# Four late tiles of layer 0's feed-forward as block products, with their sums on VectorE

## The chip, the cores and the metric

The kernel runs on one core of a Trainium2 chip. The time is the device time of one execution, in microseconds; of several executions the median counts. The profile is of one execution of its own. The engines are called by their names or by the profile's letters: TensorE (PE; its weight loads are PEld), VectorE (DVE), ScalarE (ACT), GpSimd (POOL) and SyncE (SP), whose queue issues most loads from memory.

## The reference, cut to what matters

The program computes one step of a network of two layers over 640 tokens (128 of context, 512 of the sample) with 1024 features. Each layer is a mixer (gated DeltaNet in layer 0, neighbourhood attention in layer 1) and then a gated feed-forward network. The change touches the feed-forward network of layer 0 alone:

```python
def conv_ffn(h, w_up, conv_w, conv_b, w_down):
    u = dwconv_centred(h @ w_up, conv_w) + conv_b
    val, gate = jnp.split(u, 2, axis=-1)
    return (jax.nn.silu(gate) * val) @ w_down
```

`w_up` is 1024 x 5632 (2816 value and 2816 gate columns), the convolution has three taps along the tokens, `w_down` is 2816 x 1024. The input `h` is normalised and modulated; modulation vectors of both layers come from a conditioning vector times a matrix.

## The kernel before, in words

Features lie on the 128 partitions and tokens along them, so a tile is 128 features by 640 tokens. Every matrix product is done in three passes (`pass3`, L394 to L396): each operand is split into a rounded high part and the rest (low), and high x high, high x low and low x high are added up. So every weight tile is cast to its high half on ScalarE (L382, `wh...`) and its low half is the difference, made on VectorE (L384, `wl...`). The two halves go to buffers with the tags `wh` and `wl`, two of each; loads land in a ring of two buffers, `wst`.

**The feed-forward loop (`ffn`)** goes over 22 tiles of 128 hidden features. A direct tile (`dense_pair`) computes a value tile (`duv`) and a gate tile (`dug`): 8 blocks of input features, in token pieces of 384 and 256 columns, three passes each, so 48 matmuls for each of the two. Then ScalarE and VectorE do the convolution (L454, L460), silu (L676), the product of both (L677) and the split of the result into the buffer F (L679, L680).

**Block products (`pair`).** In layer 1 the tiles 8, 10, 12, 14, 16, 18 and 20 are computed otherwise. Value and gate weights and the halves of the tokens and input features are seen as 2 x 2 blocks, and the product is made of seven block products instead of eight (Strassen's scheme in Winograd's form): seven times 4 blocks x 3 passes of 320 columns, 84 matmuls. Their order is 5, 1, 6, 3, 2, 7, 4. Sums of weight blocks (L600, L603, L604, L607, 512 columns each) and two sums of results (L610, L617, 320 columns) are on GpSimd; five sums that read a result from PSUM (L609, L612, L614, L616, L619) are on VectorE. Each of the seven weight operands is split by `quarter` (L552 on ScalarE, L553 on VectorE, 512 columns); two of them share one buffer of the tags `wh` and `wl`. Sums of the input's blocks are needed once per layer: `blocks` makes them in eight steps, which write the tiles T0 to T3; `TSTEP` says behind which tile each step is traced.

**Down products (`downs`).** After groups of tiles (`GROUPS`) the partial down projection (`rdn`) of the group is added to the residual X: eight output tiles, two token pieces each, three VectorE updates (L485) per output tile. The last group goes through `into_residual_split`, which keeps the weights of six output tiles over both token pieces (`hold`). In layer 0 the groups have 8, 7 and 7 tiles, in layer 1 they have 6, 5, 5 and 6. A group's products are traced after the tile behind it: with groups up to 8 and 15, after tiles 8 and 15.

**Modulation sums (`ada_rows`).** In layer 0's loop 64 parts are done beside the tiles: a load on GpSimd's queue (`adr`, L240, three buffers) and two multiply-and-reduce instructions on VectorE (L258) each. `SUMS[0]` says how many are traced behind each tile: none behind tile 0, then 3. The loop also issues, on GpSimd's queue, the copies that make layer 1's attention mask and bias (`rows`).

**Order.** A planner orders each engine's instructions: among those that it takes to be ready, the one traced first goes first, so a later one is pulled ahead where the engine would be idle. Each engine then works its queue in that order and waits where an operand or buffer isn't there. `high_priority` moves instructions ahead (residual updates by 300), and `chained` keeps TensorE's order as traced.

Of the kernel before, what the change touches and what calls it, by code (L numbers as in the profile page):

```python
# [13 lines left out]
F32R = mybir.dt.float32r  # L14
# [10 lines left out]
W = 640  # L25
# [29 lines left out]
ALIGN = 32, 32  # L55
SHIFT = 448
ADB = 3
GROUPS = (((0, 8), (8, 15), (15, 22)), ((0, 6), (6, 11), (11, 16), (16, 22)))
FB = 9, 7
NH = W // 2  # L60
BYBLOCK = ((), (8, 10, 12, 14, 16, 18, 20))
TSTEP = (3, 4, 4, 5, 5, 6, 6, 7)
SUMS = ((0,) + (3,) * 21, (0, 3, 3, 3, 3, 2, 2))

SEGS = ((0, PC, PC + 128, 1), (0, SC, SC + 256, 0), (1, SC + 256, SC + 512, 0))

# [26 lines left out]
class Net:  # L93
# [483 lines left out]
    def pair(self, l, i, fp, pf):  # L577

        nc, a = self.nc, self.a
        P, V = nc.gpsimd.tensor_tensor, nc.vector.tensor_tensor  # L580
        g = fp.tile([128, KT * 128], F32, tag="wsg", name=f"wsg{l}{i}", bufs=1)
        nc.sync.dma_start(g, a["w_up"][l, NFT + i])
        v = self.wp.tile([128, KT * 128], F32, tag="wst", name=f"wsv{l}{i}", bufs=WSTB)
        self.load = nc.sync.dma_start(v, a["w_up"][l, i]).ins
        v0, v1, g0, g1 = v[:, :512], v[:, 512:], g[:, :512], g[:, 512:]
        s1, s2 = (fp.tile([128, 512], F32, tag=t, name=f"{t}{l}{i}", bufs=1) for t in ("s1", "s2"))
        first, last = (lambda k: (self.hh[:, k], self.hl[:, k])), (lambda k: (self.hh[:, k + 4], self.hl[:, k + 4]))
        L, R = (0, NH), (NH, W)
# [12 lines left out]
        x = product(5, s1, self.tmov(0), L)
        nc.scalar.copy(p5, x)
        P(s2, s1, v0, ALU.subtract)  # L603
        P(g0, v0, g0, ALU.subtract)  # L604
        x = product(1, v0, first, L)
        nc.scalar.copy(p1, x)
        P(s1, v1, s2, ALU.subtract)  # L607
        x = product(6, s2, self.tmov(1), L)
        V(cg1, x, p1, ALU.add)  # L609
        P(cv1, cg1, p5, ALU.add)  # L610
        x = product(3, s1, last, R)
        V(cv1, x, cv1, ALU.add)  # L612
        x = product(2, v1, last, L)
        V(cv0, x, p1, ALU.add)  # L614
        x = product(7, g0, self.tmov(2), L)
        V(cg0, x, cg1, ALU.add)  # L616
        P(cg1, cg0, p5, ALU.add)  # L617
        x = product(4, g1, self.tmov(3), L)
        V(cg0, x, cg0, ALU.add)  # L619
        self.spare = None  # L620
        return [(0, W, cv)], [(0, W, cg)]

    def downs(self, l, grp, fs):

        g0, g1 = GROUPS[l][grp]
        n = g1 - g0
        for m in range(KT):
            w = self.weights(self.a["w_dn"][l, m][:, g0 * 128 : g1 * 128], n, f"dn{l}{grp}{m}")
            for half, c in enumerate(HALVES_R):
                ps = self.half_bank(f"rdn{l}{grp}{m}{half}", 0, half)  # L630
                self.prod(ps, -c[0], w, n, lambda k: (fs[g0 + k][:, 0], fs[g0 + k][:, 1]), c)
                with self.tc.high_priority(HP):
                    self.residual(ps, m, half, l, 5, -c[0])

    def ffn(self, l, fp, pf, norm, norms, between=None):
        nc, a = self.nc, self.a
        self.align(fp, SHIFT)
        fcw = self.smv("fcw").rearrange("p (l t w) -> p l t w", l=2, w=3)[:, l]
        fcb = self.smv("fcb").rearrange("p (l t) -> p l t", l=2)[:, l]
        last = len(GROUPS[l]) - 1  # L640

        def hold(name, n):
            if not BYBLOCK[l]:
                if name[-1] == "5":
                    return fp.tile([128, 2 * W], F32R, tag="F", name=name, bufs=FB[l])[:, 16 : 16 + n]
                return fp.tile([128, n], F32R, tag=name[:2] + name[-1], name=name, bufs=1)
            j = 2 * int(name[-1]) + (name[1] == "l")
            if j // 3 not in held:
                held[j // 3] = fp.tile([128, 2560], F32R, tag=f"T{j // 3}", name=f"Th{l}{j // 3}", bufs=1)
            o = 16 + 768 * (j % 3)  # L650
            return held[j // 3][:, o : o + n]

        g, d = (self.pa, "g", 3), (pf, "d", 5)
        direct = ((d, d), (d, d))
        self.banks = [g, d]
        if BYBLOCK[l]:
            self.T = [fp.tile([128, 2560], F32R, tag=f"T{j}", name=f"T{j}{l}", bufs=1) for j in range(4)]
            self.T = [t.rearrange("p (k a c) -> p k a c", k=4, a=2) for t in self.T]
        steps = self.blocks(fp, l)
        fs, held = {}, {}  # L660
        after = {g1: grp for grp, (_, g1) in enumerate(GROUPS[l][:-1])}
        for i in range(NFT):
            names = [f"uv{l}{i}", f"ug{l}{i}"]
            grp = after.get(i)
            if i not in BYBLOCK[l]:
                up = [a["w_up"][l, i], a["w_up"][l, NFT + i]]
                with self.behind(self.marks if i == 0 else ()):
                    pv, pg = self.dense_pair(up, names, direct, norm if i == 0 else None)
            else:
                pv, pg = self.pair(l, i, fp, pf)  # L670
            with self.tc.high_priority(FHP if i == NFT - 1 else 0):
                yv = fp.tile([128, W], F32, tag="yv", name=f"yv{l}{i}", bufs=2)
                yg = fp.tile([128, W], F32, tag="yg", name=f"yg{l}{i}", bufs=2)
                self.conv_parts(yv, pv, fcw[:, i], fcb[:, i : i + 1])
                self.conv_parts(yg, pg, fcw[:, NFT + i], fcb[:, NFT + i : NFT + i + 1])
                nc.scalar.activation(yg, yg, AF.Silu)  # L676
                nc.vector.tensor_tensor(yv, yv, yg, ALU.mult)  # L677
                f = fp.tile([128, 2 * W], F32R, tag="F", name=f"F{l}{i}", bufs=FB[l]).rearrange("p (a w) -> p a w", a=2)
                nc.scalar.copy(f[:, 0], yv)  # L679
                nc.vector.tensor_tensor(f[:, 1], yv, f[:, 0].bitcast(F32), ALU.subtract)  # L680
            fs[i] = f
            for _ in range(TSTEP.count(i) if BYBLOCK[l] else 0):
                next(steps, None)
            if between:
                between(i)
            if grp is not None:
                self.downs(l, grp, fs)
        self.spare = None
        g0, g1 = GROUPS[l][last]
        srcs = [a["w_dn"][l, m][:, g0 * 128 : g1 * 128] for m in range(KT)]  # L690
        movs = lambda k: (fs[g0 + k][:, 0, :], fs[g0 + k][:, 1, :])
        norm = self.into_residual_split(srcs, g1 - g0, movs, l, 5, f"dn{l}{last}", norms, hold, (6, 7))
        self.banks = None
        return norm
# [919 lines left out]
def build(ctx, tc, a):  # L1614
# [33 lines left out]
    with tc.tile_pool(name="fp0", bufs=2, reuse_waits="tile") as fp, ps_ffn(0) as pf:  # L1648
# [31 lines left out]
    with tc.tile_pool(name="fp1", bufs=2, reuse_waits="tile") as fp, ps_ffn(1) as pf:  # L1680
# [100 lines left out]
```

## Time and profile before

| | |
|---|---|
| median of three executions | 1844.83 us (1844.82, 1844.83, 1848.35) |
| the profiled execution | 1847.01 us, its span 1845.1 us |
| mean granted TensorE clock | 0.987 of full speed |
| layer 0's feed-forward, first direct matmul to the last group's first | 575.72 to 983.55 us |
| layer 1's feed-forward, the same | 1378.31 to 1791.95 us |
| TensorE busy, 575 to 984 us | 125.93 of 126, 55.00 of 55, 97.00 of 97, 48.00 of 48, 83.00 of 83 us |
| VectorE busy in the same stretches | 120.75, 51.93, 69.78, 21.58, 51.98 us |
| GpSimd busy in the same stretches | 21.35, 12.99, 9.41, 0.00, 0.00 us |

The stretches are tiles 0 to 8, the first group, tiles 9 to 15, the second group, and tiles 16 to 21. Rows of the profile begin with the line of the kernel or with the time from the span's start; a row of an instruction has its duration behind its start, then engine, line, operation, what it writes `<-` what it reads, the shapes, and in square brackets how long its engine was idle before it and what ended that. A busy time is the union of the instructions' durations; successive VectorE instructions overlap by about 0.1 us, so their durations add up to more.

### The profile page before, as it was taken

The page shows a single profiled execution, that of the slowest core. Times are in us where ns is not written, and L with a number is a line of the kernel's source. Part 1 is how long each engine was busy: PE and PEld are TensorE (multiplying, and loading weights), DVE is VectorE, ACT ScalarE, POOL GpSimd, SP SyncE. Part 2 cuts the span into 40 slices and gives each one's busy share as a digit, 9 for nine tenths or more (in the row PEclk, how much of TensorE's full clock was granted, in tenths as well). Part 3 has the DMA queues.
Part 4 walks back from the last instruction along what each step waited for, and adds up shares of the span by engine and source line. Part 5 has one row for each costly group of instructions (what it writes and reads, how often), then busy time and mean ns, then how long its engine had stood idle before and what let it go on. Part 6 is the DMA issues. An engine that isn't in the chain of part 4 may idle for free.

```text
span 1845.1 us, 34889 instructions
## 1 busy us (share of the span) xinstructions
PE 1774.2 (96%) x13503; PEld 1684.9 (91%) x13503; DVE 1368.7 (74%) x3445; ACT 772.0 (42%) x1606; POOL 333.4 (18%) x524
## 2 busy tenths in 40 slices
PE   6889999988999999999999999999999999999998
PEld 5878988887989999999999988888899999999998
DVE  6797868686668999965466899555679967678585
ACT  4453444254534432243233434444445424344353
POOL 0255103107003112200000212111041002032110
PEclk9999999999999999999999999999999999999999
DMA  7223233322242445542223354222233221222231
GB/s 303 74 74 110 54 126 107 100 68 79 56 160 85 154 145 174 171 157 71 80 79 93 127 153 141 76 75 68 86 128 121 86 86 63 87 71 83 79 99 60
DMA packets 103638, 194.19 MB, mean 105 GB/s; under 512 B 39624, under 2 KB 59162, under 8 KB 100712
## 3 DMA queue, kind: packets, MB, share of 16 engines
q1 hardware_dynamic: 94528, 161.57, 27.8%
q0 software_dynamic: 8400, 29.87, 5.1%
q8 instruction: 106, 1.74, 0.4%
q14 instruction: 60, 0.49, 0.1%
q10 hardware_dynamic: 544, 0.52, 0.1%
HBM read 183.09 MB, written 12.46 MB: 106 GB/s over the span
## 4 chain that ended last, share of the span: by engine, by line
PE 73%; DVE 12%; DMA 4%; issue 4%; ACT 3%; POOL 3%; SPq 1%; POOLq 0%; DVEq 0%; ACTq 0%
PE rdn L396 5%; PE rdn L394 5%; PE rdn L395 5%; PE duv L396 5%; PE duv L394 4%; PE duv L395 4%; PE dug L394 4%; PE dug L396 4%; PE dug L395 4%; PE p L982 1%; PE rgo L394 1%; PE rgo L395 1%; POOL lY L953 1%; PE rgo L396 1%; DVE nt L349 1%
## 5 line engine op out<-in xcount | busy, mean ns | idle before, releaser
L396 PE MATMUL rdn<-F,wldn 128*128 128x384 f32 (+1 forms) x632 | 193.8, 307 | 0.5 <-DVE wldn L384 0.5
L394 PE MATMUL rdn<-F,whdn 128*128 128x384 f32 (+1 forms) x632 | 193.8, 307 | 0.0
L395 PE MATMUL rdn<-F,whdn 128*128 128x384 f32 (+1 forms) x632 | 193.5, 306 | 0.0
L396 PE MATMUL duv<-hh,wluv 128*128 128x384 f32 (+1 forms) x592 | 182.0, 307 | 3.6 <-DVE wluv L384 3.6
L394 PE MATMUL duv<-hh,whuv 128*128 128x384 f32 (+1 forms) x592 | 181.5, 307 | 0.0
L395 PE MATMUL duv<-hl,whuv 128*128 128x384 f32 (+1 forms) x592 | 181.5, 307 | 0.0
L395 PE MATMUL dug<-hl,whug 128*128 128x384 f32 (+1 forms) x592 | 181.0, 306 | 0.0
L394 PE MATMUL dug<-hh,whug 128*128 128x384 f32 (+1 forms) x592 | 181.0, 306 | 0.0
L396 PE MATMUL dug<-hh,wlug 128*128 128x384 f32 (+1 forms) x592 | 181.0, 306 | 0.0
L485 DVE SCALAR_TENSOR_TENSOR X<-rdn,mods,X 128x128 f32<-128x128 f32 (+1 forms) x168 | 67.9, 435 | 79.2 <-PE rdn L396 79.0
L396 PEld LDWEIGHTS rdn<-F,wldn 128*128 128x128 f32 x632 | 118.8, 188 | 1.4 <-DVE wldn L384 1.4
L394 PEld LDWEIGHTS rdn<-F,whdn 128*128 128x128 f32 x632 | 118.6, 188 | 0.0
L395 PEld LDWEIGHTS rdn<-F,whdn 128*128 128x128 f32 x632 | 118.6, 188 | 0.0
L396 PEld LDWEIGHTS duv<-hh,wluv 128*128 128x128 f32 x592 | 111.1, 188 | 6.0 <-DVE wluv L384 5.9
L395 PEld LDWEIGHTS duv<-hl,whuv 128*128 128x128 f32 x592 | 111.2, 188 | 0.1
L396 PEld LDWEIGHTS dug<-hh,wlug 128*128 128x128 f32 x592 | 111.2, 188 | 0.0
L394 PEld LDWEIGHTS duv<-hh,whuv 128*128 128x128 f32 x592 | 111.2, 188 | 0.0
L394 PEld LDWEIGHTS dug<-hh,whug 128*128 128x128 f32 x592 | 111.1, 188 | 0.0
L395 PEld LDWEIGHTS dug<-hl,whug 128*128 128x128 f32 x592 | 111.1, 188 | 0.0
L460 DVE SCALAR_TENSOR_TENSOR yv<-duv,sm,yv 128x127 f32<-128x127 f32 (+1 forms) x222 | 86.8, 432 | 15.4 <-ACT yv L454 14.5
L382 ACT CAST whdn<-wstdn 128x896 fp32r<-128x896 f32 (+3 forms) x50 | 43.5, 869 | 126.9 <-PE rdn L395 102.4
L460 DVE SCALAR_TENSOR_TENSOR yg<-dug,sm,yg 128x127 f32<-128x127 f32 (+1 forms) x222 | 86.6, 432 | 9.1 <-ACT yg L454 8.3
(763 smaller groups left out, 5346.7 us busy)
## 6 DMA issues: line engine op xcount, KB each, us to landing
adat<-w_ada SPq DMA_DIRECT2D x20, 1024.0 KB, 5.4
adr<-w_adar POOLq DMA_DIRECT2D x80, 256.0 KB, 3.1
wstuv<-w_up SPq DMA_DIRECT2D x37, 512.0 KB, 3.5
wstug<-w_up SPq DMA_DIRECT2D x37, 512.0 KB, 3.5
adr<-w_adar SPq DMA_DIRECT2D x32, 256.0 KB, 2.8
wstdn<-w_dn SPq DMA_DIRECT2D x16, 448.0 KB, 3.3
wstdn<-w_dn SPq DMA_DIRECT2D x16, 384.0 KB, 3.1
wstdn<-w_dn SPq DMA_DIRECT2D x16, 320.0 KB, 2.9
```

The source lines that it names most:

```text
L349: nc.vector.scalar_tensor_tensor(t[:, :n], self.X[:, k, c0:c1], scg[:, k, v : v + 1], rs[:, c0 - base : c1 - base], ALU.mult, ALU.mult)
L382: nc.scalar.copy(wh[:, c], st[:, c])
L394: nc.tensor.matmul(out, a, mh, start=first, stop=False)
L395: nc.tensor.matmul(out, a, ml, start=False, stop=False)
L396: ins = nc.tensor.matmul(out, b, mh, start=False, stop=last).ins
L460: nc.vector.scalar_tensor_tensor(y[:, a:b], t[:, a + sh - lo : b + sh - lo], wv[:, tap : tap + 1], y[:, a:b], ALU.mult, ALU.add,)
L485: nc.vector.scalar_tensor_tensor(x, ps[:, base + c0 : base + c1], self.mod(l, gi, m, v), x, ALU.mult, ALU.add)
L953: eng.tensor_tensor(Y[:L, :i, lo:hi], Y[:L, :i, lo:hi], pr, ALU.add)
L982: nc.tensor.matmul(out, lhsT, rhs, start=True, stop=True, tile_position=(r, c))
```

## The change

In layer 0 the tiles 14, 16, 18 and 20 become block products too. For them all sums, those of weight blocks and of results, are on VectorE; in layer 1 GpSimd keeps its six. The eight steps of `blocks` are traced in layer 0 behind tiles 10, 10, 11, 11, 12, 12, 13 and 13. Layer 0's groups become those of layer 1 (6, 5, 5 and 6 tiles), so one group more; its F buffers go from nine to seven, and its held low and high halves of the last group go into the tiles T0 to T3, as in layer 1, instead of into tags of their own. The modulation sums of layer 0 are traced as 0, 5, 5 and then 4 behind each tile. Layer 1 computes as before.

```diff
-GROUPS = (((0, 8), (8, 15), (15, 22)), ((0, 6), (6, 11), (11, 16), (16, 22)))
-FB = 9, 7
+GROUPS = ((0, 6), (6, 11), (11, 16), (16, 22))
+FB = 7
-BYBLOCK = ((), (8, 10, 12, 14, 16, 18, 20))
-TSTEP = (3, 4, 4, 5, 5, 6, 6, 7)
-SUMS = ((0,) + (3,) * 21, (0, 3, 3, 3, 3, 2, 2))
+BYBLOCK = ((14, 16, 18, 20), (8, 10, 12, 14, 16, 18, 20))
+TSTEP = ((10, 10, 11, 11, 12, 12, 13, 13), (3, 4, 4, 5, 5, 6, 6, 7))
+SUMS = ((0, 5, 5) + (4,) * 19, (0, 3, 3, 3, 3, 2, 2))
...
     def pair(self, l, i, fp, pf):
-        P, V = nc.gpsimd.tensor_tensor, nc.vector.tensor_tensor
+        V = nc.vector.tensor_tensor
+        P = nc.gpsimd.tensor_tensor if l else V
...
     def ffn(self, l, fp, pf, norm, norms, between=None):
         def hold(name, n):
-            if not BYBLOCK[l]:
-                if name[-1] == "5":
-                    return fp.tile([128, 2 * W], F32R, tag="F", name=name, bufs=FB[l])[:, 16 : 16 + n]
-                return fp.tile([128, n], F32R, tag=name[:2] + name[-1], name=name, bufs=1)
             j = 2 * int(name[-1]) + (name[1] == "l")
...
-        if BYBLOCK[l]:
-            self.T = [fp.tile([128, 2560], F32R, tag=f"T{j}", name=f"T{j}{l}", bufs=1) for j in range(4)]
-            self.T = [t.rearrange("p (k a c) -> p k a c", k=4, a=2) for t in self.T]
+        self.T = [fp.tile([128, 2560], F32R, tag=f"T{j}", name=f"T{j}{l}", bufs=1) for j in range(4)]
+        self.T = [t.rearrange("p (k a c) -> p k a c", k=4, a=2) for t in self.T]
...
-            for _ in range(TSTEP.count(i) if BYBLOCK[l] else 0):
+            for _ in range(TSTEP[l].count(i)):
                 next(steps, None)
```

The remaining lines replace `GROUPS[l]` by `GROUPS` and `FB[l]` by `FB`.

More of the change, by code (lines that the diff above doesn't have):

```diff
@@ L623, in downs @@
     def downs(self, l, grp, fs):
-        g0, g1 = GROUPS[l][grp]
+        g0, g1 = GROUPS[grp]
         n = g1 - g0
@@ L639, in ffn @@
         fcb = self.smv("fcb").rearrange("p (l t) -> p l t", l=2)[:, l]
-        last = len(GROUPS[l]) - 1
+        last = len(GROUPS) - 1
         def hold(name, n):
-            if not BYBLOCK[l]:
-                if name[-1] == "5":
-                    return fp.tile([128, 2 * W], F32R, tag="F", name=name, bufs=FB[l])[:, 16 : 16 + n]
-                return fp.tile([128, n], F32R, tag=name[:2] + name[-1], name=name, bufs=1)
             j = 2 * int(name[-1]) + (name[1] == "l")
@@ L655, in ffn @@
         self.banks = [g, d]
-        if BYBLOCK[l]:
-            self.T = [fp.tile([128, 2560], F32R, tag=f"T{j}", name=f"T{j}{l}", bufs=1) for j in range(4)]
-            self.T = [t.rearrange("p (k a c) -> p k a c", k=4, a=2) for t in self.T]
+        self.T = [fp.tile([128, 2560], F32R, tag=f"T{j}", name=f"T{j}{l}", bufs=1) for j in range(4)]
+        self.T = [t.rearrange("p (k a c) -> p k a c", k=4, a=2) for t in self.T]
         steps = self.blocks(fp, l)
         fs, held = {}, {}
-        after = {g1: grp for grp, (_, g1) in enumerate(GROUPS[l][:-1])}
+        after = {g1: grp for grp, (_, g1) in enumerate(GROUPS[:-1])}
         for i in range(NFT):
@@ L677, in ffn @@
                 nc.vector.tensor_tensor(yv, yv, yg, ALU.mult)
-                f = fp.tile([128, 2 * W], F32R, tag="F", name=f"F{l}{i}", bufs=FB[l]).rearrange("p (a w) -> p a w", a=2)
+                f = fp.tile([128, 2 * W], F32R, tag="F", name=f"F{l}{i}", bufs=FB).rearrange("p (a w) -> p a w", a=2)
                 nc.scalar.copy(f[:, 0], yv)
@@ L688, in ffn @@
         self.spare = None
-        g0, g1 = GROUPS[l][last]
+        g0, g1 = GROUPS[last]
         srcs = [a["w_dn"][l, m][:, g0 * 128 : g1 * 128] for m in range(KT)]
```

## The prediction

> **What bounds the kernel now.** I read the page first (busy shares, chain of waits), then windows cut at the first matmul of each piece of work, then VectorE's groups and the order of single instructions around one pair of block products. Layer 0 has no such pair before the change, but layer 1 has seven, built by the same function, so its rows are the price list.
>
> ```profile
> PE 1774.2 (96%) x13503; PEld 1684.9 (91%) x13503; DVE 1368.7 (74%) x3445; ACT 772.0 (42%) x1606; POOL 333.4 (18%) x524
> ...
> PE 73%; DVE 12%; DMA 4%; issue 4%; ACT 3%; POOL 3%; SPq 1%; POOLq 0%; DVEq 0%; ACTq 0%
> ```
>
> TensorE is busy 96% of the span and carries 73% of the chain. The next windows have, after the stretch and its length, PE, weight loads, VectorE, ScalarE and GpSimd busy, then the granted clock. The first four are layer 0: a direct tile, the 8-tile down group, a direct tile after the modulation sums have ended, the 7-tile group. The others are layer 1: tile 6, the 6-tile group, pair 14, direct tile 15, the 5-tile group behind pair 16, tile 19, tile 21 (behind pairs 18 and 20).
>
> ```profile
> core 0: us, PE busy (x) PEld busy (x) DVE busy (x) ACT busy (x) POOL busy (x), PEclk, DMA share, GB/s
> 618.82:632.58 13.76, 13.76 (x99) 13.76 (x98) 13.55 (x33) 5.73 (x8) 2.19 (x4) 1.00 0.46 154
> 701.38:756.42 55.04, 55.04 (x387) 55.04 (x386) 52.01 (x128) 10.35 (x11) 12.61 (x24) 1.00 0.57 183
> 797.79:811.55 13.76, 13.76 (x99) 13.76 (x97) 8.54 (x16) 5.74 (x8) 0.00 (x0) 1.00 0.35 114
> 852.83:900.99 48.16, 48.16 (x339) 48.16 (x337) 21.58 (x38) 9.48 (x11) 0.00 (x0) 1.00 0.27 81
> 1462.57:1477.11 14.54, 14.30 (x99) 13.99 (x98) 14.17 (x31) 7.03 (x12) 0.00 (x0) 1.00 0.24 69
> 1477.11:1520.21 43.10, 42.74 (x290) 42.19 (x289) 25.39 (x52) 10.08 (x14) 0.00 (x0) 1.00 0.31 92
> 1649.47:1661.79 12.32, 12.32 (x86) 12.32 (x85) 11.06 (x22) 7.44 (x12) 1.47 (x2) 1.00 0.27 82
> 1661.79:1676.77 14.98, 14.16 (x98) 13.84 (x97) 12.82 (x19) 6.18 (x9) 7.00 (x5) 1.00 0.20 62
> 1689.09:1724.13 35.04, 34.85 (x243) 34.53 (x241) 21.79 (x41) 8.54 (x11) 2.58 (x2) 1.00 0.32 92
> 1750.20:1764.92 14.72, 14.13 (x98) 13.81 (x97) 12.56 (x18) 6.17 (x9) 6.99 (x5) 1.00 0.21 74
> 1777.24:1791.95 14.71, 14.12 (x98) 13.80 (x97) 12.63 (x22) 8.40 (x11) 1.72 (x1) 1.00 0.48 133
> ```
>
> In layer 0 TensorE never waits: every direct tile takes 13.76 us at clock 1.00, even where VectorE is busy 13.55 of it, and the 7-tile group takes 7 x 6.88. So layer 0's time is its matmuls, and only fewer matmuls, or a new wait, can move it. In layer 1 pair 14 takes 12.32 us, but the piece behind each pair is longer than it would be alone.
>
> **What a pair costs and gives back.** A direct tile has 96 matmuls, a pair 84 of 320 columns. Per pair 13.76 - 12.32 = 1.44 us is removed; four pairs: **5.76 us**. [...]
>
> What is given back lies right behind each pair. These rows (start, duration, engine, line) are the end of layer 1's pair 14 and the start of tile 15; the first one is an F split with nothing beside it, from an earlier pair:
>
> ```profile
> 1558.04 0.82 DVE L680 TENSOR_TENSOR F<-yv,F 128x640 fp32r<-128x640 f32 x1 [0.79 <-ACT F L679]
> ...
> 1656.25 1.19 POOL L610 TENSOR_TENSOR cv<-cg,p 128x320 f32<-128x320 f32 x1 [6.51 <-DVE cg L609]
> ...
> 1656.62 1.50 DVE L680 TENSOR_TENSOR F<-yv,F 128x640 fp32r<-128x640 f32 x1
> 1658.05 0.48 DVE L612 TENSOR_TENSOR cv<-pp,cv 128x320 f32<-128x320 f32 x1
> 1658.45 0.68 DVE L553 TENSOR_TENSOR wlp<-wsg,whp 128x512 fp32r<-128x512 f32 x1
> 1659.05 0.48 DVE L614 TENSOR_TENSOR cv<-pp,p 128x320 f32<-128x320 f32 x1
> 1660.52 1.01 DVE L460 SCALAR_TENSOR_TENSOR yv<-cv,sm,yv 128x127 f32<-128x127 f32 x2 [0.99 <-ACT yv L454]
> 1661.45 0.48 DVE L616 TENSOR_TENSOR cg<-pp,cg 128x320 f32<-128x320 f32 x1
> 1661.85 1.22 DVE L384 TENSOR_TENSOR wluv<-wstuv,whuv 128x1024 fp32r<-128x1024 f32 x1
> ...
> 1660.39 1.04 ACT L382 CAST whuv<-wstuv 128x1024 fp32r<-128x1024 f32 x1
> ...
> 1663.12 0.44 PE L396 MATMUL duv<-hh,wluv 128*128 128x384 f32 x1 [0.82 <-DVE wluv L384]
> ```
>
> The next tile's halves take buffers that the pair's seven quarters occupied, so the cast starts only when the sixth of seven products has ended, one product (12.32/7 = 1.76 us) before the pair does: 1661.79 - 1.76 = 1660.03. Cast and split are 1.04 + 1.22 = 2.26 us, more than 1.76 plus the two matmuls that need the high half alone, so TensorE stands at the third, which starts at 1663.12. With the split right behind the cast (1661.43 instead of 1661.85) 0.4 us less is lost. Layer 0 gets its pairs at 14, 16, 18 and 20, where layer 1 has pairs too, with the same pieces behind them, and the windows price these: tile 15 14.98 - 13.76 = 1.22; the 5-tile group 35.04 - 5 x 6.88 = 0.64; tile 19 14.72 - 13.76 = 0.96; tile 21 0.95. **Given back: 3.77 us.**
>
> **The sums on VectorE.** Four of 512 and two of 320 columns per pair go to VectorE instead of GpSimd. VectorE's groups in layer 1 (count | busy, mean ns | idle before) give their price and what GpSimd's sums cost VectorE now:
>
> ```profile
> L460 DVE SCALAR_TENSOR_TENSOR yg<-cg,sm,yg 128x127 f32<-128x127 f32 (+1 forms) x28 | 21.8, 836 | 0.0
> ...
> L460 DVE SCALAR_TENSOR_TENSOR yv<-cv,sm,yv 128x127 f32<-128x127 f32 (+1 forms) x28 | 17.2, 655 | 6.9 <-ACT yv L454 6.9
> ...
> L680 DVE TENSOR_TENSOR F<-yv,F 128x640 fp32r<-128x640 f32 x14 | 15.6, 1113 | 4.1 <-ACT F L679 4.0
> ...
> L619 DVE TENSOR_TENSOR cg<-pp,cg 128x320 f32<-128x320 f32 x7 | 3.4, 492 | 6.6 <-POOL cg L617 6.6
> ```
>
> Added per pair, by the rows of 512 and 320 columns above: 4 x 0.68 + 2 x 0.48 = 3.7 us, or 3.2 by starts (the next instruction starts 0.60 after the 512 at 1658.45 and 0.40 after the 320 at 1658.05). Taken away: a short and a long convolution step take 1.01 us together undisturbed, but 21.8/14 = 1.56 for the gate and 17.2/14 = 1.23 for the value; twice each per pair, 1.5 us. F takes 0.82 alone and 1.11 in the mean of two, 0.6 us. L619's wait for GpSimd is 6.6/7 = 0.9. Together 3.0 us: VectorE is left about even. The F at 1656.62 takes 1.50 because GpSimd's sum of L610 runs from 1656.25: without it L612 comes 0.68 earlier, with that sum on VectorE's own queue 0.40 later.
> [...]
> At the boundary, the sum of L617 (0.40) can stand ahead of the split, and the 0.68 - 0.40 = 0.28 gained above is ahead too. I take 0; the ends are +0.4 us a pair (L617 in front, nothing gained) and -0.4 (split right behind the cast).
>
> **The blocks.** Eight steps at tiles 10 to 13: VectorE gets per two steps two sums of 640 columns (as F, 0.82) and eight of 320: 1.64 + 3.84 = 5.5 us; ScalarE gets four casts of 320, beside 5.74 of 13.76 busy. A direct tile there keeps VectorE busy 8.54 of 13.76, so 5.2 are free, and the group behind tile 11 leaves more (21.58 of 48.16 busy in the group shown). I take 0. The other end is layer 1, where block steps and modulation sums met: tile 6 and the next group lost 0.78 and 43.10 - 41.28 = 1.82, so **0 to 2.6**. A gain is excluded, since layer 0 has no wait to lose.
>
> **What else moves.** The fourth down group adds no matmul (22 tiles in all), but 24 residual updates:
>
> ```profile
> L485 DVE SCALAR_TENSOR_TENSOR X<-rdn,mods,X 128x128 f32<-128x128 f32 (+1 forms) x168 | 67.9, 435 | 79.2 <-PE rdn L396 79.0
> ```
>
> 24 x 0.435 = 10.4 us of VectorE beside TensorE's matmuls, hidden by the idle of the groups; uncovered in the first group, 52.01 of 55.04 was busy and TensorE still lost nothing. The modulation sums are due 26 parts by tile 6, up from 18. In the trace, one adj instruction per part, 25 have started by the end of tile 6, because the planner fills idle VectorE with them:
>
> ```profile
> 575.72:673.86 98.14, 18.59 (x25) 1.00 0.42 133
> ```
>
> So the new quota asks for what happens anyway, and I take 0; if parts push weight splits back, that is C below. Seven quarter splits (7 x 0.68 = 4.8) replace two of 1.22, covered as in layer 1. The pair's two loads replace the tile's two on SP's queue, same bytes; GpSimd's queue keeps its loads and gets nothing new. Seven F buffers and low halves held in the T tiles: layer 1's last group works so; 0. Leaving layer 0 I take 0, between -0.5 and +0.5.
>
> **Sum.** -5.76 + 3.77 = -1.99 us. The profiled execution took 1847.01 us (1.9 of it outside its span), so it would take 1845.0. It lies 2.2 above the median of 1844.83, and the median becomes **1842.8 us**. One execution in three of before was at 1848.35, so about 0.2% (3.7 us) is what a measurement can tell from no change.
>
> **Rivals.**
> A, faster: the wait behind a pair shrinks, since VectorE is freed of GpSimd. By the bound above 0.4 less at four places gives -3.6, 1841.2; with none left -5.76, 1839.1. For it: 3.0 us of disturbance per pair goes. Against it: cast and split alone exceed the last product. [...] Chance 0.16.
> B, slower: VectorE becomes the bound inside the pairs. Its busy time over pair 14 and tile 15 is 11.06 + 12.82 = 23.9 of 27.3; with 3.2 more and 2.1 less of disturbance 25.0. The last product's split ends at 1659.13 and its product starts at 1660.03, a slack of 0.90. If the five sums ahead of it (4 x 0.60 + 0.40 = 2.8) come with no idle time to take them up, TensorE waits 1.9 per pair: 4 x 1.9 - 1.99 = +5.6, 1850.4. It decides from the point where more than 0.90 us of sums delays a split. Against it: s1, s2 and g0 can run as the loads land, before the pair. Chance 0.17.
> C, block steps and modulation sums together keep VectorE from the weight splits and lose 2.6 as in layer 1: -1.99 + 2.6 = +0.6, 1845.4. For it: tile 6 of layer 1 has VectorE busy 14.17 of 14.54. Against it: the steps stand four tiles later than the bulk of the sums. Chance 0.08. That the change does nothing is excluded: the engine and the tiles are written in the code.
>
> **Numbers.** The forecast (waits as in layer 1) has 0.59, its own range -1.99 +/- 1.6, 1841.2 to 1844.4. C lies within 0.2%, and so does nearly all of the forecast, of which 0.01 goes over to faster and 0.02 to slower: faster 0.17, same 0.64, slower 0.19. The range takes in half of A's stretch and the part of B up to a wait of 1.5 per pair (4 x 1.5 - 1.99 = +4.0): 1840.2 to 1848.8.
>
> **What would show it.** Right: pairs of about 12.3 us in layer 0, TensorE waiting once behind each for the split of L384, 0.4 to 1.1 us; L680 at 0.82 there; direct tiles 0 to 13 at 13.76. Wrong: TensorE waiting for wlp (L553) inside a pair (B), tiles 10 to 13 or the group behind tile 11 longer (C), no wait behind the pairs (A), or a time beyond 3.7 us either way.

## The result, and the profile after

The changed kernel takes 1870.62 us (median of four executions, 1867.58 to 1873.0), the kernel before 1846.59 us on the same chip (1844.82 to 1850.77): ratio 1.0116, interval 1.0089 to 1.0143. By that ratio it is slower by some 21 us, by the two medians by 24, either way far beyond the upper end of the range. The profiled execution took 1869.32 us, where the prediction's sum gave 1845.0: 24.3 us more.

These are windows of the changed kernel with the columns of the prediction: tiles 3 and 4, the 6-tile group, the 5-tile group behind tile 11, tile 12, pair 14, tile 15, the group behind pair 16, tiles 19 and 21, the last group, the stretch from the end of the last group to layer 1's loop, and layer 0's loop up to the last group.

```profile
618.04:633.63 15.59, 14.16 (x98) 13.84 (x97) 15.11 (x38) 5.97 (x9) 2.73 (x5) 1.00 0.47 153
633.63:648.65 15.02, 14.16 (x98) 13.85 (x97) 14.46 (x35) 5.62 (x8) 2.69 (x5) 1.00 0.47 157
676.75:718.02 41.27, 41.27 (x290) 41.27 (x289) 40.78 (x101) 10.09 (x14) 7.11 (x13) 1.00 0.53 166
786.83:822.21 35.38, 34.56 (x243) 34.36 (x241) 22.35 (x52) 7.97 (x11) 4.32 (x8) 1.00 0.54 179
822.21:837.26 15.05, 14.41 (x96) 14.09 (x97) 8.27 (x15) 3.90 (x5) 0.00 (x0) 1.00 0.33 106
851.30:863.62 12.32, 12.32 (x86) 12.32 (x85) 9.89 (x20) 7.44 (x12) 0.00 (x0) 1.00 0.27 86
863.62:881.60 17.98, 15.61 (x99) 15.29 (x97) 13.40 (x25) 6.31 (x9) 0.00 (x0) 0.91 0.18 49
893.91:930.28 36.37, 34.69 (x242) 34.37 (x241) 22.15 (x43) 8.40 (x11) 0.00 (x0) 1.00 0.31 88
956.36:977.41 21.05, 16.80 (x98) 16.48 (x97) 15.19 (x31) 6.17 (x9) 1.70 (x3) 0.84 0.40 124
989.74:1004.53 14.79, 14.03 (x98) 13.71 (x97) 13.18 (x23) 8.32 (x11) 0.00 (x0) 1.00 0.47 134
1004.53:1052.24 47.71, 43.08 (x302) 42.72 (x301) 37.12 (x84) 18.25 (x34) 7.64 (x6) 1.00 0.29 93
1052.24:1399.76 347.52, 334.81 (x2544) 300.32 (x2545) 248.27 (x699) 157.92 (x376) 67.29 (x107) 0.99 0.34 106
575.07:1004.53 429.46, 416.56 (x2846) 413.42 (x2845) 358.59 (x793) 162.09 (x244) 43.37 (x74) 0.99 0.38 119
```

The pairs take 12.32 us, as forecast, so their 5.76 us are won. Everything else that moved is a loss, each measured against the price of the piece before (13.76 for a direct tile, 6.88 per tile of a group):

- tiles 3 to 6: 15.59, 15.02, 14.05 and 14.05, so 3.7 more; forecast 0;
- the second group and tiles 12 and 13 (15.05 and 14.04): 0.98 + 1.57 = 2.6 more; forecast 0, bounds 0 to 2.6;
- behind the pairs: tile 15 4.2, the group 2.0, tile 19 7.3, tile 21 1.0, tile 17 nothing: 14.5; forecast 3.8;
- last group and attention: the same two windows of before are 50.14 and 344.62; a tile less in the group leaves 50.14 - 6.88 = 43.26, so 4.45 + 2.90 = 7.35 more; forecast 0.

These are 3.7 + 2.6 + 10.7 + 7.35 = 24.3 us, the whole difference. The waits of TensorE over the stretch (time, times, longest) say for what:

```profile
PE duv L396 <- DVE wluv L384: 10.3, 6, 4.3
PE dqn L394 <- DVE X L485: 3.4, 1, 3.4
PE nrs L322 <- POOL nst L314: 1.7, 2, 1.2
PE rdn L396 <- DVE wldn L384: 1.7, 1, 1.7
PE duv L394 <- ACT whuv L382: 0.8, 1, 0.8
```

Seven are waits for a first weight split on VectorE, three belong to the norm and attention's first product (`dqn`) at the end, and one is for tile 12's first cast on ScalarE. None is inside a pair. In the loop they are 12.8 us, and 20.8 are lost there. Of the rest some 4.9 come with a halved clock behind the waits of tiles 15 and 19 (below); some 3 are a slower pace of TensorE at full clock, which the last section describes: tiles 5, 6 and 13 take 14.05, 14.05 and 14.04 without any wait.

In `pair` the lines of the changed kernel are one higher than before: its L618 and L620 are L617 and L619 of the kernel before. Here is VectorE's queue at the end of pair 14, with the cast of tile 15's weights on ScalarE and the matmul that waits:

```profile
861.96 1.05 ACT L382 CAST whuv<-wstuv 128x1024 fp32r<-128x1024 f32 x1
...
862.57 0.74 DVE L460 SCALAR_TENSOR_TENSOR yv<-cv,sm,yv 128x511 f32<-128x511 f32 x1
863.23 0.48 DVE L618 TENSOR_TENSOR cg<-cg,p 128x320 f32<-128x320 f32 x1
863.63 0.35 DVE L460 SCALAR_TENSOR_TENSOR yv<-cv,sm,yv 128x127 f32<-128x127 f32 x1
864.17 0.49 DVE L620 TENSOR_TENSOR cg<-pp,cg 128x320 f32<-128x320 f32 x1 [0.19 <-DVE yv L460]
864.57 0.74 DVE L460 SCALAR_TENSOR_TENSOR yv<-cv,sm,yv 128x511 f32<-128x511 f32 x1
865.23 1.22 DVE L384 TENSOR_TENSOR wluv<-wstuv,whuv 128x1024 fp32r<-128x1024 f32 x1
...
866.50 0.44 PE L396 MATMUL duv<-hh,wluv 128*128 128x384 f32 x1 [2.37 <-DVE wluv L384]
```

The cast ends at 863.01, the split starts at 865.23: 2.22 us later, behind two sums of the pair and its convolution. In layer 1 it was 0.42 (prediction). One of the sums, L620, reads the pair's last product, so the split of the next tile's weights, which needs nothing of it, stands behind the pair's very end. In front of tile 19 it is worse. Three modulation parts, six instructions of L258 of which one is shown, stand between the sums, and the split starts 4.10 us after its cast's end at 955.75:

```profile
956.77 0.75 DVE L258 CUSTOM_DVE_ANT_0 adj<-adr,cb,adh 128x512 f32<-128x512 f32 x1
...
958.52 0.49 DVE L620 TENSOR_TENSOR cg<-pp,cg 128x320 f32<-128x320 f32 x1
...
959.85 1.22 DVE L384 TENSOR_TENSOR wluv<-wstuv,whuv 128x1024 fp32r<-128x1024 f32 x1
```

**The two longest waits of the loop cost more than their length.** Tile 15 waits 2.37 and loses 4.2; tile 19 waits 4.25 and loses 7.3. The first two windows are the six microseconds behind these two waits; the third column from the end is the granted clock. The third window is the 3.41 us of tile 15 in which it is halved:

```profile
866.00:872.00 6.00, 5.50 (x23) 5.50 (x24) 5.97 (x10) 1.47 (x2) 0.00 (x0) 0.72 0.50 142
961.00:967.00 6.00, 5.88 (x19) 5.88 (x20) 4.57 (x9) 0.74 (x1) 0.00 (x0) 0.53 0.78 245
867.65:871.06 3.41, 3.41 (x12) 3.41 (x12) 3.38 (x5) 1.47 (x2) 0.00 (x0) 0.50 0.57 154
```

By an estimate from the last row, 3.41 us at half the clock cost 1.7 us; tile 15 loses 1.84 more than it waits. At tile 19 the clock is halved for twice as long, from 959.81 to 966.64, the end of the wait included, and the loss is 3.04 above the wait. Behind waits of 1.4 and 1.7 us (tile 3, the group behind pair 16) the clock stays at 1.00 and the loss, 1.8 and 2.0, is close to the wait.

**Where the modulation sums went.** Starts of L258's adj, one per part, are counted in windows of before (prediction: 25 in tiles 0 to 6; 31 more by the end of the first group, 9 after it) and of the changed kernel:

```profile
575.07:676.75 101.68, 19.43 (x26) 1.00 0.41 129
676.75:822.21 145.46, 23.27 (x31) 1.00 0.49 155
822.21:944.04 121.83, 0.00 (x0) 0.99 0.24 74
944.04:963.00 18.96, 2.25 (x3) 0.92 0.36 109
1004.53:1052.24 47.71, 2.98 (x4) 1.00 0.29 93
```

57 parts are done by tile 12, then none for 122 us, three in pair 18, four in the last group. There they hold back the norm:

```profile
1033.67 0.56 POOL L240 DMA_DIRECT2D adr<-w_adar  x1 [73.60 <-DVE adh L258]
1033.97 0.16 DVE L313 TENSOR_SCALAR nst<-nps 128x3 f32<-128x3 f32 x1
1035.83 2.67 DVE L258 CUSTOM_DVE_ANT_0 adr<-adr,cb,sm 128x512 f32<-128x512 f32 x1
1038.44 2.61 DVE L299 TENSOR_TENSOR nacc<-nacc,nsq 128x256 f32<-128x256 f32 x1
```

TensorE's sums for the norm (`nps`) end at 1032.59, but L313, which reads them, stands behind two instructions of L258 and starts 1.38 us later; in the kernel before it was 0.04. Then an instruction of a part and the next sum of the norm take 2.67 and 2.61 us beside GpSimd's first splits for attention (1035.57 to 1040.76), where the one otherwise takes 0.75 and a larger sum of the norm (384 columns) 0.56, and the normalised values (L349) start only at 1040.97. GpSimd itself stood 73.6 us at one load that waited for a late part, with the norm's power (L314, at 1034.26) behind it, but that cost next to nothing: the load was out of the way at 1034.23, and L313, for which the power has to wait too, ended at 1034.13.

### The profile page after: what moved, and what is told of

The parts are those of the page before. It is cut to its first block, busy times and chain, and to the rows that moved or that the text cites. A ratio compares the mean times of both kernels' runs of the same rounds, so it can differ in the third digit from the quotient of the medians.

```text
span 1867.6 us, 34982 instructions
## 1 busy us (share of the span) xinstructions
PE 1778.5 (95%) x13455; PEld 1686.7 (90%) x13455; DVE 1417.7 (76%) x3565; ACT 789.2 (42%) x1650; POOL 337.2 (18%) x524
## 4 chain that ended last, share of the span: by engine, by line
PE 66%; DVE 16%; DMA 6%; issue 4%; ACT 4%; POOL 3%; SPq 1%; POOLq 0%; DVEq 0%; ACTq 0%
PE rdn L396 4%; PE rdn L395 4%; PE rdn L394 4%; PE duv L396 4%; PE dug L394 4%; PE dug L395 4%; PE dug L396 4%; PE duv L395 4%; PE duv L394 4%; PE p L978 1%; PE rgo L394 1%; DVE adr L258 1%; PE rgo L395 1%; DVE adj L258 1%; PE rgo L396 1%
## 5 line engine op out<-in xcount | busy, mean ns | idle before, releaser
L396 PE MATMUL duv<-hh,wluv 128*128 128x256 f32 (+1 forms) x528 | 165.9, 314 | 13.7 <-DVE wluv L384 13.7
L396 PE MATMUL rdn<-F,wldn 128*128 128x256 f32 (+1 forms) x560 | 171.7, 307 | 2.2 <-DVE wldn L384 2.2
L394 PE MATMUL rdn<-F,whdn 128*128 128x256 f32 (+1 forms) x560 | 171.5, 306 | 0.0
L395 PE MATMUL rdn<-F,whdn 128*128 128x256 f32 (+1 forms) x560 | 171.4, 306 | 0.0
L394 PE MATMUL duv<-hh,whuv 128*128 128x256 f32 (+1 forms) x528 | 164.5, 312 | 0.8 <-ACT whuv L382 0.8
L395 PE MATMUL duv<-hl,whuv 128*128 128x256 f32 (+1 forms) x528 | 164.2, 311 | 0.0
L396 PE MATMUL dug<-hh,wlug 128*128 128x256 f32 (+1 forms) x528 | 162.2, 307 | 0.0
L394 PE MATMUL dug<-hh,whug 128*128 128x256 f32 (+1 forms) x528 | 162.2, 307 | 0.0
L395 PE MATMUL dug<-hl,whug 128*128 128x256 f32 (+1 forms) x528 | 162.2, 307 | 0.0
L240 POOL DMA_DIRECT2D adr<-w_adar x80 | 43.9, 549 | 491.3 <-DVE mods L258 233.3
L485 DVE SCALAR_TENSOR_TENSOR X<-rdn,mods,X 128x256 f32<-128x256 f32 (+1 forms) x192 | 77.8, 436 | 70.0 <-PE rdn L396 69.7
L460 DVE SCALAR_TENSOR_TENSOR yv<-duv,sm,yv 128x127 f32<-128x127 f32 (+1 forms) x198 | 77.7, 434 | 12.8 <-ACT yv L454 12.5
```

Source lines behind the costliest of these rows:

```text
L240: queue.dma_start(w, src)
L394: nc.tensor.matmul(out, a, mh, start=first, stop=False)
L395: nc.tensor.matmul(out, a, ml, start=False, stop=False)
L396: ins = nc.tensor.matmul(out, b, mh, start=False, stop=last).ins
L460: nc.vector.scalar_tensor_tensor(y[:, a:b], t[:, a + sh - lo : b + sh - lo], wv[:, tap : tap + 1], y[:, a:b], ALU.mult, ALU.add,)
L485: nc.vector.scalar_tensor_tensor(x, ps[:, base + c0 : base + c1], self.mod(l, gi, m, v), x, ALU.mult, ALU.add)
```

## The experiments

Theory O (order): the split behind a pair is late because VectorE's queue has the pair's last sums ahead of it. Theory P (parts): the new quota puts modulation parts where VectorE has no room, in tiles 3 to 6 and at the end. Theory R (room): VectorE has too much work in this loop; it is busy 315 of 408 us before and 359 of 429 after, 43 us more, so that relief in one place returns in another. The row of before for the loop up to the last group (that of the changed kernel is the last of its windows):

```profile
575.72:983.55 407.83, 407.76 (x2847) 407.31 (x2845) 315.16 (x689) 145.18 (x201) 43.75 (x75) 1.00 0.40 126
```

Rivals: the block steps that were pulled into early tiles, and the groups. Ratios are to the kernel before on the same chip. The table gives, for each run that keeps the pairs, what each piece lost in the profiled execution against the prices above (the pairs against 12.32; "end" is last group and attention), in us. Each row is a single execution, that of e1 8.5 us above the median of its run, those of e5, e6 and e13 some 4:

| run | ratio (interval) | tiles 3-6 | group 1 | tiles 7-11 | group 2, tiles 12, 13 | pairs | behind pairs | end |
|---|---|---|---|---|---|---|---|---|
| the change | 1.0116 (1.0089-1.0143) | 3.7 | 0 | 0 | 2.6 | 0 | 14.5 | 7.4 |
| e1 | 1.0102 (1.0074-1.0130) | 3.7 | 1.1 | 1.9 | 4.2 | 2.2 | 2.8 | 13.3 |
| e2 | 1.0116 (1.0100-1.0132) | 2.6 | 0 | 0 | 7.4 | 10.5 | 6.5 | 5.0 |
| e3 | 1.0078 (1.0059-1.0097) | 2.6 | 0 | 0 | 6.4 | 10.7 | 2.9 | 2.4 |
| e5 | 1.0196 (1.0163-1.0229) | 3.5 | 0 | 0 | 0.8 | 13.4 | 29.0 | 2.6 |
| e6 | 1.0071 (1.0045-1.0098) | 0 | 10.0 | 1.9 | 1.8 | 0 | 4.7 | 6.0 |
| e7 | 1.0067 (1.0045-1.0089) | 0 | 9.4 | 0 | 2.0 | 0 | 2.9 | 6.6 |
| e8 | 1.0111 (1.0081-1.0141) | 0 | 8.0 | 10.0 | 1.7 | 1.9 | 3.1 | 4.3 |
| e9 | 1.0079 (1.0060-1.0099) | 0 | 0 | 1.6 | 7.5 | 4.2 | 2.1 | 4.4 |
| e12 | 1.0077 (1.0056-1.0098) | 1.1 | 7.5 | 0 | 0 | 0 | 6.6 | 6.1 |
| e13 | 1.0069 (1.0044-1.0094) | 0 | 11.4 | 0 | 0 | 0 | 3.5 | 7.1 |

**e1: the split first.** The first casts and splits of tiles 15, 19 and 21 and of the group behind pair 16 are moved ahead by priority; nothing else.

```diff
+        with self.tc.high_priority(300 if name in ("uv015", "uv019", "uv021", "dn020") else 0):
             nc.scalar.copy(wh[:, c], st[:, c])
...
```

> The changed kernel with one thing altered: the weight split of the piece behind each pair (tiles 15, 19, 21 and the first down weight of the second-last group) gets a higher priority, so that it stands ahead of the pair's last two sums in VectorE's queue. Trace of the changed kernel: 14.4 us are lost behind the four pairs (4.2, 2.0, 7.2, 1.0), 14.5 us elsewhere. Order theory (the split waits behind sums that need the pair's last product): behind the pairs it falls to 4 to 5 us, the time by 9 to 10 us, to about 1861. Rival (VectorE is simply too full, the order does not matter): the time stays within 3 us of the changed kernel, and the waits move to the splits of the second halves. Rival (late modulation sums): tile 19 keeps at least 3 us of its 7.2, and the time falls by 6 at most.

The order is what was late: the split now starts 0.22 us after its cast, ahead of the pair's sum (the lines of the kernel are one higher here).

```profile
873.54 1.22 DVE L385 TENSOR_TENSOR wluv<-wstuv,whuv 128x1024 fp32r<-128x1024 f32 x1
874.68 0.48 DVE L619 TENSOR_TENSOR cg<-cg,p 128x320 f32<-128x320 f32 x1
```

Behind the pairs 2.8 us are lost instead of 14.5, less than the 3.8 of layer 1's rows. But the time hardly falls. The parts that stood in front of tile 19 now come behind its split, and VectorE is late for pair 20, where TensorE waits 1.8 us for wlp: the mechanism of rival B, once. The last group and attention lose 13.3 instead of 7.4. O is shown for its place; the late parts stayed (three in tile 19, four in the last group).

**e2 and e3: block steps held.** In e2 each pair of block steps is held behind the F split of its tile; e3 is e1 and e2 together.

```diff
-            for _ in range(TSTEP[l].count(i)):
-                next(steps, None)
+            with self.behind((done,) if l == 0 else ()):
+                for _ in range(TSTEP[l].count(i)):
+                    next(steps, None)
```

> The changed kernel with the block steps held in VectorE's queue behind the F split of the tile they are traced at (tiles 10 to 13), instead of being pulled forward to tiles 0 to 10; by the planned order 63 of the 64 modulation parts then stand before tile 13 instead of 57. Late-sums theory (the early steps take VectorE's idle time, and the parts that are pushed back wait in the way at pair 18, in the last group and in GpSimd's queue): tiles 3 to 6 lose nothing (3.7 us now), tile 19 3 us less, the last group's second half and the start of the attention 8 us less; time about 1856, tiles 12 and 13 unchanged or 1 us worse. Order theory alone: only what lies behind the pairs matters, so no more than 3 us fall, to 1868.

> Both alterations together. If the two causes are separate and complete, about 22 us fall and the kernel stands 2 us below the one before (1844 to 1846 on the same scale), as the forecast of -2 had it with waits of layer 1's size behind the pairs. If they are one and the same cause, it is no better than the better of the two.

Tiles 3 to 6 still lose 2.6 with no block step near them, so the early steps are not their main cause. The parts now end earlier and the last group takes 42.65 instead of 47.71. The price is new: at tiles 10 to 13 the steps do not fit, and pair 14 stands for its T operands (windows of e2: the second group, pair 14):

```profile
788.21:829.41 41.20, 37.13 (x243) 36.30 (x241) 30.92 (x70) 9.83 (x15) 3.54 (x6) 0.96 0.52 167
857.49:880.31 22.82, 14.67 (x86) 13.91 (x85) 18.04 (x37) 9.27 (x16) 0.00 (x0) 0.78 0.14 47
```

So the prediction's "5.2 are free" at tiles 10 to 13 was wrong for steps held where they are traced; in the changed kernel they were pulled forward. e3 keeps both: little behind the pairs (2.9), much at pair 14 (10.7), so the two repairs do not add up to the 22 us of its expectation.

**e4: groups only.** The change without pairs and block steps, with the old quota.

```diff
-BYBLOCK = ((14, 16, 18, 20), (8, 10, 12, 14, 16, 18, 20))
+BYBLOCK = ((), (8, 10, 12, 14, 16, 18, 20))
-SUMS = ((0, 5, 5) + (4,) * 19, (0, 3, 3, 3, 3, 2, 2))
+SUMS = ((0,) + (3,) * 21, (0, 3, 3, 3, 3, 2, 2))
```

(and no block steps in `TSTEP[0]`.)

> No block products, no block steps and the old quota of modulation parts in layer 0; only the groups of 6, 5, 5 and 6 tiles with seven F buffers and the held halves in the T tiles. My forecast took 0 for these: within 1 us of the kernel before. Rival (the extra group's residual updates and fewer F buffers cost part of the loss): 3 us or more slower, lost in the down groups.

Ratio 1.0034 (1.0012 to 1.0056): the groups alone cost some 6 us. Its last group and attention take 42.66 and 350.06, 4.8 more than before: about two thirds of the end's 7.4 come without any pair, though one late part stands in this last group too. As these are single executions, a difference of 1 us means nothing there: e14 below, with the groups of before and shorter parts, takes 49.53 and 346.29, 1.1 more than before. The profiled execution of e4 lies 3.3 above its median, and 5.2 of its loss is the slower pace in tiles 1 to 11 and the first group.

**e5: the sums back on GpSimd.**

```diff
-        P = nc.gpsimd.tensor_tensor if l else V
+        P = nc.gpsimd.tensor_tensor
```

> Only the sums go back to GpSimd in layer 0; pairs, block steps, groups and quota stay as in the change. Theory 'order' (with the sums on VectorE its queue has the next tile's split behind the pair's last sums): the split of L384 stands ahead of them again, the five pieces behind the pairs (tile 15, group, tiles 17, 19, 21) lose about 4 us in all instead of 14.5, and as all 64 parts of the modulation sums are planned by tile 16, the last group and the start of attention get back some 5 to 8; ratio to the kernel before 1.001 to 1.005. Rival 'block steps and quota': the sums' engine matters little, the pieces behind the pairs keep over 10 us, ratio 1.009 to 1.012.

A miss for both theories: 1.0196. Putting the sums back on GpSimd does not cure the change; it makes it worse, here. Its queue holds the parts' loads, and pair 14, tile 15 and pair 16 take 16.63, 34.41 and 21.36 us. The waits of GpSimd over the three, and those of SP's queue:

```profile
POOL adr L240 <- DVE mods L258: 23.4, 2, 21.9
POOL cv L611 <- DVE cg L610: 22.5, 2, 13.5
```

```profile
SPq L368 <- DVE wlp L553: 63.0, 2, 45.0
```

A sum waits behind a load, the load for a part, the part stands behind splits, and the next load of weights waits 45 us for a buffer that such a split has to free. Behind pairs 18 and 20, where no part is left, tiles 19 and 21 take 14.76 and 14.62, as in layer 1.

**e6: parts early.** Only the quota is another.

```diff
-SUMS = ((0, 5, 5) + (4,) * 19, (0, 3, 3, 3, 3, 2, 2))
+SUMS = ((0, 3, 3, 3, 3, 3, 20, 5, 5, 5, 5, 5, 5) + (2,) * 9, (0, 3, 3, 3, 3, 2, 2))
```

> The change with another quota of modulation sums, nothing else: 0, 3, 3, 3, 3, 3, 20, 5, 5, 5, 5, 5, 5, then 2 parts behind the tiles, so that all 64 are planned by tile 12 (57 in the change, the last four in the last group). Theory 'late parts': tile 19 loses 4 to 5 us less, the last down group takes about 42.7 instead of 47.7, attention starts some 4 us earlier, tiles 3 to 6 lose under 1 instead of 3.7; about 14 less in all, ratio 1.002 to 1.006. The waits for the split behind the pairs stay: about 10 us. Rival (parts end on time anyway, the order alone is the cause): less than 4 us change, ratio 1.009 to 1.012.

The windows of tile 3 and the first group:

```profile
620.49:634.25 13.76, 13.76 (x99) 13.76 (x97) 13.51 (x33) 5.98 (x9) 2.15 (x4) 1.00 0.44 147
675.53:726.82 51.29, 45.36 (x290) 44.73 (x289) 49.30 (x124) 9.69 (x13) 10.49 (x20) 0.93 0.53 173
```

Tiles 3 to 6 lose nothing: their 3.7 us are the quota's. It is not the amount of work: tile 4 of the changed kernel has eight instructions of L258, four parts, as many as tile 3 of before with its 13.55 of 13.76 busy, and yet it took 15.02. What differs is where the parts stand. These are the cast of tile 3's first weights, an instruction of a part, and the split in the changed kernel; then the split of the same weights before, where the cast ended at 613.07:

```profile
611.99 1.04 ACT L382 CAST whuv<-wstuv 128x1024 fp32r<-128x1024 f32 x1
613.24 0.74 DVE L258 CUSTOM_DVE_ANT_0 adr<-adr,cb,sm 128x512 f32<-128x512 f32 x1
...
618.71 1.22 DVE L384 TENSOR_TENSOR wluv<-wstuv,whuv 128x1024 fp32r<-128x1024 f32 x1
```

```profile
613.26 1.22 DVE L384 TENSOR_TENSOR wluv<-wstuv,whuv 128x1024 fp32r<-128x1024 f32 x1
```

Before, the split followed its cast by 0.19 us, with the parts behind it; after, six instructions of parts that are due stand ahead of it, and it comes 5.68 us after its cast, 0.67 after tile 3's first matmul.

Behind the pairs 4.7 are left, which is nearly what was forecast, with the sums on VectorE all the same: with the parts out of the way, the queue's order at the pairs' ends is another too (the split starts 1.28 us after its cast before tile 15 and 0.61 before tile 19, where it was 2.22 and 4.10). The 20 parts at tile 6, however, fill VectorE in the first group (49.30 of 51.29), and that group loses the 10 us.

**e7, e8, e9: both repairs, then other places.** e7 is the quota of e6 with e1's splits first. e8 moves and holds the block steps too, e9 spreads the quota.

```diff
 e8: TSTEP[0] = (8, 8, 9, 9, 10, 10, 12, 12), held as in e2
 e9: SUMS[0]  = (0, 3, 3, 3, 3, 3, 9) + (7,) * 6 + (0,) * 9, parts from the 50th on by priority
```

> The quota of e6 and the split of the first weights behind each pair (tiles 15, 19, 21 and the group) ahead of the pair's last sums on VectorE, as in e1. If the two causes are separate and complete, both gains add up: pieces behind the pairs lose about 2.5 us, the last group 42.7, tiles 3 to 6 under 1; the pairs' 5.8 us are left over, minus block steps: ratio 0.997 to 1.001. If a third cost is hidden (block steps, one group more), ratio 1.003 or more and it shows in tiles 7 to 13 or the second group.

> As e7, and the eight steps of the block sums are traced behind tiles 8, 8, 9, 9, 10, 10, 12, 12 and held behind the F split of their tile, so that none is pulled into tiles 0 to 7. If early steps cost nothing the time is that of e7 within 2 us; if they are what delays tiles 3 to 6, those lose nothing and it is 1 to 3 us faster; if held steps collide with the splits of the second group, as in e2, that group takes 36 or more instead of 34.4 to 35.4 and it is slower by the same.

> As e7, but the quota of modulation sums is 0, 3, 3, 3, 3, 3, 9, then 7 behind each of six tiles, the parts from the 50th on are moved ahead by priority, and so 20 parts instead of 25 lie between tiles 6 and 7 (19 in the change). Theory: what is left of the slow-down in e7 is 9.4 us in the first down group (20 parts of quota ahead of its weight splits) and 5 to 7 us at the passage from the last group to attention, which all kernels with a last group of 6 tiles have; with the first group back at about 41.3 the time is 8 to 10 us below e7's, ratio 1.000 to 1.003. Rival (VectorE simply has too much work in this loop, and relief in one place returns in another): the first group stays short but tiles 7 to 13, the second group or the pieces behind pairs grow by 5 or more, ratio 1.005 or more.

In e7 both repairs hold where they were made (tiles 3 to 6 nothing, behind pairs 2.9), and the first group keeps its 9.4. e8 is slower than e7: the held steps, from 761.0 us on, stand ahead of the split of tile 10's first weights (769.19), TensorE waits 5.5 us for it, and that tile takes 22.09. In e9 that group is repaired (41.28), and the second one takes 41.92 and pair 16 16.53: the rival of its expectation held. The waits of ScalarE from 780 to 830 us of e9, the second group, show how:

```profile
ACT whdn L385 <- DMA wstdn<-w_dn: 10.3, 2, 7.1
ACT T L573 <- DVE bv L567: 4.4, 2, 4.1
```

A cast of a block sum stood 4.1 us for VectorE's bv, with the casts of the group's weights behind it in ScalarE's queue, and one of these 7.1 us for its load. Which of the two came first was not tried.

**e10, e11: the end.** The kernel before, with groups of 6, 5, 4 and 7 tiles (e10) and of 8, 8 and 6 (e11).

> The kernel before with four groups in layer 0, of 6, 5, 4 and 7 tiles: one group more than before, but the last as long as before; no pairs, no block steps, sums as before. Theory 'short last group' (a last group of 6 tiles has 3.3 us fewer products behind the norm of its first half, and VectorE's chain of norm work is not covered): the passage from the last group to attention costs nothing against before, the last group takes about 50 and attention up to layer 1's loop 344 to 346; ratio 0.999 to 1.001. Rival 'four groups' (24 more residual updates cost the time): ratio 1.002 to 1.004 as in e4.

> The kernel before with three groups in layer 0, of 8, 8 and 6 tiles: no group more, but a last one of 6 tiles. Theory 'short last group': last group about 42.7 and the stretch from attention to layer 1's loop 348 to 350 instead of 344.6, so 3 to 5 us slower, ratio 1.001 to 1.003. Rival 'four groups': ratio 0.999 to 1.001.

Ratios 1.0013 (1.0001 to 1.0026) and 1.0010 (0.9992 to 1.0029): about 2 us each at most, and not told apart. Last group and attention take 2.8 us more than before in e10 and 6.6 in e11, whose profiled execution (1862.48) was the longest of its ten. The theory of the short last group had wanted none in e10. Which property of the groups costs the end its 5 us stays open.

**e12, e13, e14: less work.** Each modulation sum is cut to 64 of its 512 columns (the rest is left out), instructions and loads stay: in the change (e12), with e1's splits first (e13), and in the kernel before (e14).

```diff
+            c0 = n - 64 if (l, m) in ((0, 5), (1, 0), (1, 1), (1, 2)) else 0
...
-                    junk, w, self.cb[:, v, h * n : h * n + n], 1.0, init, ALU.mult, ALU.add, out
+                    junk[:, c0:], w[:, c0:], self.cb[:, v, h * n + c0 : h * n + n], 1.0, init, ALU.mult, ALU.add, out
```

> The change with the modulation sums of layer 0's loop cut to 64 of 512 columns each: as many instructions, loads and waits, but some 70 us less of VectorE's work (the rest of each sum is left out). Theory 'VectorE has no room' (VectorE is busy 359 us of the changed loop's 429 and 309 of 401 before; work placed at one spot is missing at another): without this load direct tiles take 13.76, the three inner groups 41.28 + 34.40 + 34.40 within 1.5 in all, the pieces behind the pairs lose 4 to 6 us together as in e6, and only the passage to attention keeps 3 to 6; ratio 1.000 to 1.003. Rival 'order alone' (the split behind the pair's sums, whatever the load): the pieces behind the pairs keep over 10 us, ratio 1.005 or more.

> As e12, with the first split behind each pair ahead of the pair's last sums (as in e1). By both theories the pieces behind the pairs lose about 2.5 us; what is left of the pairs' gain is then 3.2 minus the passage to attention: ratio 0.999 to 1.001. If it is 1.004 or more, a cost is left that neither VectorE's load nor this order explains.

> The kernel before with the same cut modulation sums: as no wait of its layer 0 comes from them, the time is that of before within 0.15%; this is the base of e12 and e13.

What R asks for is seen in the middle of the loop: with most of the load gone the second group, tiles 7 to 13 and the pairs lose nothing, and behind the pairs 6.6 are left, or 3.5 with the split first. The runs do not prove R all the same: a shorter part also holds back a split for less time, so that they cannot tell load from order. And R fails for the first group, by a cause that none of the theories had: short parts are queued more densely than their loads land, and VectorE waits for them, splits queued behind (waits of VectorE from 655 to 712 us of e12):

```profile
DVE adj L259 <- DMA adr<-w_adar: 12.8, 11, 2.5
```

The same happened to the base: e14 is at 1.0028 (1.0011 to 1.0045), not at 1.000, its tiles 4 to 8 taking 14.67 to 16.87. So e12 shows less than it was meant to: the work as such is one cause, a part queued ahead of its load another.

## Why the prediction was wrong, point by point

**The pairs' gain** was right: 12.32 us each, 5.76 in all. So were the direct tiles ahead of tile 3, and the low chance of TensorE waiting for wlp inside a pair: the changed kernel shows none. The side of rival B came, its mechanism did not. C's mechanism, parts that keep VectorE from the weight splits, came, but in tiles 3 to 6 and in front of tile 19, not where C had it.

**"I take 0; the ends are +0.4 us a pair"** for the sums on VectorE is the step that failed. It looked at L617's sum alone (L618 of the changed kernel). The planner put L618, L620 and the pair's convolution ahead of the split, 2.2 us of queue where 0.42 was assumed, and in front of tile 19 parts too, 4.1 us; e1 takes them away, and the loss falls from 14.5 to 2.8. Layer 1's waits were a price list for layer 1's order only.

**"The new quota asks for what happens anyway, and I take 0"** failed too. 25 parts in tiles 0 to 6 were counted rightly, and the changed kernel has 26; but a part that is due stands ahead of the next split, where a part pulled into idle time stood behind it. 3.7 us in tiles 3 to 6 (e6), and the late parts in front of tile 19 and in the last group, were not seen as possible.

**The blocks**: at the second group and tiles 12 and 13, where the prediction looked for their price, 2.6 us were lost, its upper end. That this is the steps' price is not shown. 1.1 of it is the slower pace, the planner had pulled the steps forward into tiles 0 to 11, and e12, with the same steps and short parts, loses nothing there. Held at their tiles they cost 17 us (e2: 6.8 and 10.5).

**"VectorE is left about even"** was a local sum. Over the loop it got 43 us more work; it had 93 us free before, but in the late tiles and groups, not where it was needed.

**Leaving layer 0, "between -0.5 and +0.5"**, was 7.35: about 5 with the groups (e4), the rest, by the rows above, with late parts.

**The prices from layer 1** were read as waits alone, and only partly were. In the rows behind its pairs TensorE is idle 0.82 + 0.19 + 0.59 + 0.59 = 2.2 of the 3.77 us; the other 1.6 is the slower pace (14.16 us busy in tile 15, where a direct tile needs 13.76). Of C's 2.6 only 0.24 + 0.36 = 0.6 is idle time. Nor did the cast in front of tile 15 start when the sixth product ended (1660.03): it came at 1660.39, right behind a convolution step of 0.92 us that ScalarE had begun at 1659.56. And the waits behind which the clock fell to 0.50 cost more than any of these rows could show (4.2 for 2.37, 7.3 for 4.25).

No version beat the kernel before: 5.8 us won, less 2.1 to 3.5 behind the pairs with the split first, less 2.4 to 13.3 at the end, leaves about 1 us at best, before what the other pieces lose is paid for.

## What to carry to other kernels

When work moves to an engine that also feeds the bottleneck and works its queue in order, as VectorE did here (the split for tile 15 started 2.22 us after its cast had ended, behind sums queued ahead of it), price what will stand ahead of the feeding instruction in its queue, and not only the busy time; rows from another place give that price only if the order there is the same. The same holds for background work: giving it an earlier due time can change nothing in its amount and still put it ahead of the instruction that feeds the bottleneck. Read the idle time of that engine piece by piece. And avoid long waits of the matrix engine: behind the three of 2.37, 3.40 and 4.25 us in the changed kernel the clock was 0.72, 0.74 and 0.53 in the mean of the next six us.

## What the runs showed of the hardware

The clock fell after short waits. The changed kernel has three waits of TensorE of over 2 us between 575 and 1075 us: behind 2.37 us (tile 15) it was 0.72 over the next six us, behind 4.25 us (tile 19) 0.53, and behind 3.40 us (attention's first product, at 1052.24) 0.74. In the experiments the windows with waits of 2.4 us (pair 16 of e9), 3.4 us (second group of e9), 5.6 us (first group of e6) and 7.1 us (pair 14 of e2) have a mean clock of 0.90, 0.96, 0.93 and 0.78. In shorter waits the length alone does not decide: 1.79 us, in the first group of e13, was followed by a clock of 0.72 (the row below), while 2.08 us (tile 15 of e12, which took 16.12) left it at 1.00:

```profile
684.57:690.57 6.00, 6.00 (x30) 6.00 (x31) 5.96 (x19) 2.19 (x3) 1.08 (x2) 0.72 0.60 197
```

Apart from that, TensorE at a granted clock of 1.00 showed two paces: 13.76 us for a direct tile, or 14.13, for many tiles in a row, without any wait, as in tile 4 of e4 (13.76 again from its tile 12 on):

```profile
637.41:651.55 14.14, 14.14 (x99) 14.14 (x97) 13.07 (x31) 5.63 (x8) 2.02 (x4) 1.00 0.46 148
```

In e11 it set in at a wait: tile 10 waits 0.8 us, and tiles 11 to 21 take 14.13 each. In e4 it is there from tile 1 on without one. What starts and ends it was not tried, and as each kernel has one trace, it is not shown whether it differs between executions of the same kernel.
